# SyncE's loads of the differential heads in written order, with their tiles laid out anew and the clearing moved to VectorE

## The chip, the cores and the metric

The kernel runs on one core of one Trainium2 chip. A core has TensorE (PE, with PEld for the loading of the stationary operand), VectorE (DVE), ScalarE (ACT), GpSimd (POOL) and SyncE (SP, which only issues transfers here). The metric is the device time of one execution in microseconds (us); lower is better. Before the change the median of 3 runs is 2444.63 us (2444.59 to 2448.08).

## The reference, cut to what matters

One layer of a diffusion transformer over 512 latent tokens and 256 context tokens, model width 2048, all in float32. Eight differential attention heads and eight latent-attention heads run on one modulated RMS norm; their outputs go through one projection, and a gated MLP with a short convolution follows. The change lies in the differential heads:

```python
def _diff_attend(q, k, v, lam):
    q1, q2 = jnp.split(q, 2, axis=-1)
    k1, k2 = jnp.split(k, 2, axis=-1)
    s1 = jnp.einsum('bhqd,bhkd->bhqk', q1, k1).astype(jnp.float32) * DA_SCALE
    s2 = jnp.einsum('bhqd,bhkd->bhqk', q2, k2).astype(jnp.float32) * DA_SCALE
    w = jax.nn.softmax(s1, axis=-1) - lam * jax.nn.softmax(s2, axis=-1)
    return jnp.einsum('bhqk,bhkd->bhqd', w.astype(v.dtype), v)
```

Queries are the 512 latent tokens, keys and values all 768 tokens; a head is 128 wide, and q1, q2 and k1, k2 are its halves. Queries and keys carry a rotary embedding.

## The kernel before

**Precision.** A float32 operand is used as two parts, high and low (`split`, lines 75 to 84: a cast on ACT at L80, a subtraction on DVE at L81), and a product as three matmuls (`mm3`, L104 to L106).

**Stages.** Modulation and norms; projections of keys, latent inputs and values, which go to DRAM (`k_d`, `v_d`, `q0_d`; keys by L389, values by L470, the second half of the values through POOL's queue); the differential heads, which are the stage of the change; the latent-attention heads; output projection; MLP. The projection of the values for the second half of the heads is the last work before the differential heads, and the tiles of that time (pools `kv` and `kvs`) are given back when they begin. The pool `da` of the differential heads takes over their memory: `cb1` (8 KB a partition, read by the products with the modulation weights until shortly before), `lt`, `rt`, `qs` and `nq` and others of the latent norms and of the first queries, then the two buffers of the modulation weights, then `kh` and `kl`, through which the values are evacuated. `reuse_waits="tile"` makes a new tile wait only for the old tiles that lie under it.

**One differential head** (`da_head`). Its keys' high parts (`ks`, two buffers), low parts (`klz`, two tiles, used in turn) and values (`v`, two buffers) are loaded. `klz` holds each half's low part in its own 64 partitions and zeros in the other 64; the zeros are written once, by four instructions on POOL (L506). For each of four tiles of 128 queries and each of the two maps, four matmuls make the scores in PSUM (L482, two buffers), DVE takes the maximum (L484), ACT the exponential (L486); then DVE, POOL and DVE normalise and combine the two maps (L538, L539, L540). After the four tiles, for each of six blocks of 128 keys, PE transposes the weights (L494, one PSUM buffer), ACT and DVE split them, and three matmuls add their product with the values (`po`, L104 to L106). ACT copies the sum to `o` (L497), and SP stores it to `o_d` (L544).

**The queries of a head** (`da_queries`). Those of head 0 were made earlier and are loaded from `q0_d` (L515). For the others `feature` multiplies two blocks of query weights (512 KB each) with the 16 tiles of the normed input, 48 matmuls into the PSUM tile `f`; DVE applies the rotary embedding (L149 to L152), and ACT and DVE scale and split (L395, L396). A block is loaded by SP and split by `wblock` (L90). The helper `ahead` runs two blocks ahead in the written program: at the end of `feature` of one head it writes down the loads for the next head. The raw blocks have three buffers (`wr`), the split ones three each (`wh`, `wl`).

**What sets the order.** The program is written head by head,

```python
    for h in range(NH):
        da_head(h, da_queries(h))
```

but a planner decides the order on each engine: at each moment of its own timeline it takes, of the instructions that are ready, the first in written order. On the chip each engine then runs its instructions in that fixed order and waits at each for its semaphores. So a load that is written late can be issued early, if its buffer is free, and PE's instructions of several heads are mixed. Inside a `tc.manual_schedule(engines={...})` block the named engines keep the written order; the last stages of the kernel before use it for PE, ACT, DVE and SP.

Of the kernel before, what the change touches and what calls it, by code (L numbers as in the profile page):

```python
# [9 lines left out]
F32 = mybir.dt.float32  # L10
F32R = mybir.dt.float32r
# [6 lines left out]
P = 128  # L18
D = 2048
KT = D // P  # L20
T = 512
C = 256
TT = T + C
GRID_W = 64
NH = 8
# [7 lines left out]
NKEY = TT // P  # L33
# [19 lines left out]
def layer_kernel(ctx: ExitStack, tc: tile.TileContext, small, rope, c_row, cc_row, x_t, ctx_t, ada, ada_k,  # L53
                 w_g0, w_f, w_v, w_uqn, w_uqr, w_ukv, w_o, w_up0, w_up, w_dn, out_t):
    nc = tc.nc
    pe, ve, sc, gp = nc.tensor, nc.vector, nc.scalar, nc.gpsimd
# [8 lines left out]
    def nm(s):  # L65
        n[0] += 1
        return f"{s}{n[0]}"
# [6 lines left out]
    def b_tile(tag="b", bufs=None):  # L74
        return ps_b.tile([P, 512], F32, tag=tag, name=nm(tag), bufs=bufs or nb[0])
# [62 lines left out]
    q0_d = dram.tile([2, P, T], F32, name="q0_d")  # L138
# [5 lines left out]
    k_d = [dram.tile([2, P, TT], F32, name=f"k_d{h}") for h in range(NH)]  # L144
    v_d = [dram.tile([4, P, 2, NKEY, P], F32, name=f"v_d{i}") for i in range(2)]

    def apply_rope(out, ps, tmp):
        t2 = tmp()
        ve.tensor_tensor(out, ps, ropet[:, 0, :], op=ALU.mult)  # L149
        ve.stream_shuffle(t2, ps, mask=[i ^ 16 for i in range(32)])  # L150
        ve.tensor_tensor(t2, t2, ropet[:, 1, :], op=ALU.mult)
        ve.tensor_tensor(out, out, t2, op=ALU.add)  # L152
# [41 lines left out]
    for row, wide in ((c_row, cb), (cc_row, ccb)):  # L194
        nc.sync.dma_start(wide[0:1], row)
        sc.activation(wide[0:1], wide[0:1], AF.Silu)
        for j in range(0, D, 512):
            t = b_tile()
# [104 lines left out]
    for i in range(2):  # L303
        o = OFF["lam"] + 128 * i
# [11 lines left out]
    for kt in range(KT):  # L316
# [5 lines left out]
        o = (kt % 2) * C  # L322
        hx.append((a2k(F32R), a2k(F32R)))
        hc.append((chh[:, o:o + C], chl[:, o:o + C]))
        with tc.high_priority():
            h = st.tile([P, TT], F32, tag="h", name=nm("h"), bufs=3)
            for i, (x, c, m, (hh, hl)) in enumerate(((xs[kt], slice(0, T), modx, hx[kt]),
                                                     (ct, slice(T, TT), modc, hc[kt]))):
                b, t, r = m[:, kt:kt + 1], h[:, c], rinv[:, c]
# [61 lines left out]
    def stacked_queries(pool, q, scale, bufs=2):  # L391

        qs = [pool.tile([P, T], F32R, tag=f"qs{i}", name=nm("qs"), bufs=bufs) for i in range(2)]
        for i, (r, o) in enumerate(((lo, hi), (hi, lo))):
            sc.mul(qs[i][r], q[r], scale)  # L395
            ve.scalar_tensor_tensor(out=qs[i][o], in0=q[r], scalar=scale, in1=qs[i][r].bitcast(F32),  # L396
                                    op0=ALU.mult, op1=ALU.subtract)
        return qs
# [19 lines left out]
    for i in range(2):  # L418
        t = kv.tile([P, TT], F32, tag="lt", name=nm("ckv"), bufs=3)
# [9 lines left out]
    def feature(lat, ctxo):  # L429
        for hf in range(2):  # L430
            wh, wl = next_block()
            for j in range(8):
                kt = hf * 8 + j
                w = (wh[:, j * P:(j + 1) * P], wl[:, j * P:(j + 1) * P])
                mm3(lat, w, hx[kt], kt == 0, kt == KT - 1)
                if ctxo is not None:
                    mm3(ctxo, w, hc[kt], kt == 0, kt == KT - 1)
        ahead(2)
# [8 lines left out]
    for i in range(3):  # L447
        lat = b_tile()
        feature(lat, None)
        t = kv.tile([P, TT], F32, tag="lt", name=nm("cq"), bufs=3)[:, :T]  # L450
# [4 lines left out]
    for half in range(2):  # L455
        s0, s1, b0, b1_ = s_tile(), s_tile(), b_tile(), b_tile()
        vo = [s0[:, :512], s0[:, 512:], s1[:, :512], s1[:, 512:], b0, b1_]
        for kb in range(8):
            wh, wl = next_block()
            for j in range(2):  # L460
                kt = kb * 2 + j
                w = (wh[:, j * 512:(j + 1) * 512], wl[:, j * 512:(j + 1) * 512])
                for t in range(NKEY):
                    src, o = (hx[kt], t * P) if t < 4 else (hc[kt], (t - 4) * P)
# [13 lines left out]
    def scores_softmax(mms, pool, tag, bufs, l):  # L478
        s = s_tile()
        for c0, c1 in ((0, T), (T, TT)):  # L480
            for i, (a, b) in enumerate(mms):
                pe.matmul(s[:, c0:c1], a, b[:, c0:c1], start=i == 0, stop=i == len(mms) - 1)  # L482
        m = sm.tile([P, 1], F32, tag="m", name=nm("m"), bufs=4)
        ve.tensor_reduce(out=m, in_=s[:, :TT], axis=AX.X, op=ALU.max, negate=True)  # L484
        p = pool.tile([P, TT], F32, tag=tag, name=nm(tag), bufs=bufs)
        sc.activation(p, s[:, :TT], AF.Exp, bias=m, accum_out=l)  # L486
        return p

    def weighted_values(pool, ws, v, dst, last=False):
        po = b_tile("po", 1)  # L490
        for kt in range(NKEY):
            pt = b_tile("f", 2) if last and kt % 3 else b_tile("pt", 1)
            for qt in range(NQT):
                pe.transpose(pt[:, qt * P:(qt + 1) * P], ws[qt][:, kt * P:(kt + 1) * P], ident)  # L494
            wth, wtl = split_tiles(pool, ("wth", "wtl"), [P, T], 2, pt)
            mm3(po, v(kt), (wth, wtl), kt == 0, kt == NKEY - 1)
        sc.copy(dst, po)  # L497


    da = tc.alloc_tile_pool(name="da", bufs=1, reuse_waits="tile")  # L500


    klz = [da.tile([P, 2, TT], F32R, name=nm("klz")) for _ in range(2)]
    for t in klz:
        for i, r in enumerate((hi, lo)):
            gp.memset(t[r, i].bitcast(F32), 0.0)  # L506

    def da_rtmp():
        return da.tile([P, T], F32, tag="rt", name=nm("rt"), bufs=2)

    def da_queries(h):
        if h == 0:
            qs = [da.tile([P, T], F32R, tag=f"qs{i}", name=nm("qs"), bufs=2) for i in range(2)]
            for i in range(2):
                nc.sync.dma_start(qs[i].bitcast(F32), q0_d[i])  # L515
            return qs
        lat = b_tile("f", 2)
        feature(lat, None)
        q = da_rtmp()
        apply_rope(q, lat, da_rtmp)  # L520
        return stacked_queries(da, q, DA_SCALE)

    def da_head(h, qs):
        ks = da.tile([P, 2, TT], F32R, tag="ks", name=nm("ks"), bufs=2)
        kl = klz[h % 2]
        for i, r in enumerate((lo, hi)):
            nc.sync.dma_start(ks[r].bitcast(F32), k_d[h][0].rearrange("(i p) n -> p i n", i=2))
            nc.sync.dma_start(kl[r, i].bitcast(F32), k_d[h][1][r])
        v = da.tile([P, 2, NKEY, P], F32R, tag="v", name=nm("v"), bufs=2)
        nc.sync.dma_start(v.bitcast(F32), v_d[h // 4][h % 4])  # L530
        ws = []
        for qt in range(NQT):
            c = slice(qt * P, (qt + 1) * P)
            l = sm.tile([P, 2], F32, tag="l", name=nm("l"), bufs=4)
            ps = [scores_softmax([(qs[i][:, c], ks[:, i]), (qs[i][:, c], kl[:, i])], da, f"p{i}", (8, 3)[i],
                                 l[:, i:i + 1]) for i in range(2)]
            rl = sm.tile([P, 2], F32, tag="rl", name=nm("rl"), bufs=4)
            ve.reciprocal(rl, l)  # L538
            gp.tensor_scalar(out=ps[1], in0=ps[1], scalar1=rl[:, 1:2], scalar2=neglam, op0=ALU.mult, op1=ALU.mult)  # L539
            ve.scalar_tensor_tensor(out=ps[0], in0=ps[0], scalar=rl[:, 0:1], in1=ps[1], op0=ALU.mult, op1=ALU.add)  # L540
            ws.append(ps[0])
        o = da.tile([P, T], F32, tag="o", name=nm("o"), bufs=2)
        weighted_values(da, ws, lambda kt: (v[:, 0, kt], v[:, 1, kt]), o)
        nc.sync.dma_start(o_d[h], o)  # L544

    for h in range(NH):
        da_head(h, da_queries(h))
    ap_.release()


# [78 lines left out]
    for h in range(NH):  # L629
        i = h % 2  # L630
        if i == 0:
            qs, qn, kn, vs = nxt
# [753 lines left out]
```

## Time and profile before

| what | value |
|---|---|
| median of 3 runs | 2444.63 us |
| the profiled execution | 2446.12 us |
| its span, first to last instruction | 2444.3 us |
| mean granted TensorE clock | 0.99 |
| PE, DVE, ACT, POOL busy | 97%, 71%, 46%, 9% |
| from the end of the value projection to the end of the differential heads | about 478 to 704 us |
| stores of the eight heads' results begin | 538.4 to 701.3 us |

The span is cut into windows, and a view of windows gives for each engine the busy time and, in brackets, the number of instructions. PE's matmuls are pipelined, so that a full row for PE is not yet PE at its peak. In a view of waits each line says which engine's instruction waited for which, for how long in total, how often, and the longest. A row in order of time gives start and duration; "x6" means that rows next to each other were merged, and a duration with the waits inside it is then the whole stretch. "SPq" is SyncE's queue: its rows are the issues of transfers, not the transfers. In groups by line, the two numbers after the bar are the busy time in us and the mean of one instruction in ns.

### The profile page before, as it was taken

The numbers are of one execution on the slowest core, as the hardware profiler recorded it, in microseconds if no ns is written. First come the engines' busy times: TensorE is split into PE (matmuls) and PEld (weight loads), VectorE is DVE, ScalarE is ACT, GpSimd is POOL, SyncE is SP. The second block draws the span as 40 slices with busy tenths as digits, with TensorE's granted clock in tenths as the row PEclk, the third lists the DMA queues.
The fourth block names the chain that finished last, engine by engine and source line by source line (L and its number), as shares of the span: only waits on it lengthen the run. The fifth ranks groups of instructions, "written<-read, shape, count | busy, mean of one in ns | idle before, by whom it ended". The sixth has DMA issues, their size and how long they took to land.

```text
span 2444.3 us, 32956 instructions
## 1 busy us (share of the span) xinstructions
PE 2374.6 (97%) x12790; PEld 1987.4 (81%) x12790; DVE 1730.4 (71%) x2304; ACT 1116.3 (46%) x1700; POOL 221.0 (9%) x244
## 2 busy tenths in 40 slices
PE   7999999999999999999999999999999999999998
PEld 3778887877777778889888888888888888888887
DVE  4668786388868877369766666666666666666667
ACT  4342121155545542245545454545454545454545
POOL 0000000121100002100111111111111111111110
PEclk9999999999999999999999999999999999999999
DMA  7867899555411139523555555565556555555573
GB/s 276 275 238 293 308 339 325 178 179 138 140 59 44 44 147 332 176 87 113 137 140 135 141 135 142 134 143 133 143 132 143 133 141 134 140 135 141 133 191 106
DMA packets 130708, 403.33 MB, mean 165 GB/s; under 512 B 14323, under 2 KB 25075, under 8 KB 122099
## 3 DMA queue, kind: packets, MB, share of 16 engines
q1 hardware_dynamic: 104118, 350.87, 43.8%
q0 software_dynamic: 25280, 49.30, 11.6%
q8 instruction: 100, 1.64, 0.3%
q10 hardware_dynamic: 1152, 1.05, 0.1%
q14 instruction: 58, 0.48, 0.1%
HBM read 331.68 MB, written 69.48 MB: 164 GB/s over the span
## 4 chain that ended last, share of the span: by engine, by line
PE 83%; DVE 8%; ACT 3%; DMA 3%; issue 2%; POOL 1%; SPq 0%; DVEq 0%; ACTq 0%; POOLq 0%
PE y L1105 12%; PE b L104 10%; PE b L105 10%; PE b L106 10%; PE z L1105 6%; PE y L1107 6%; PE z L1107 3%; PE s L104 3%; PE s L105 3%; PE s L106 3%; PE s L482 3%; PE x L1105 2%; DMA ada<-in_ada 1%; PE x L1107 1%; PE f L104 1%
## 5 line engine op out<-in xcount | busy, mean ns | idle before, releaser
L961 DVE TENSOR_TENSOR wl<-wr,wh 128x1024 fp32r<-128x1024 f32 x144 | 176.4, 1225 | 157.1 <-ACT wh L953 156.5
L953 ACT CAST wh<-wr 128x1024 fp32r<-128x1024 f32 x144 | 151.0, 1049 | 233.3 <-PE b L105 119.5
L104 PE MATMUL b<-ah,wh 128*128 128x512 f32 (+1 forms) x664 | 256.8, 387 | 0.0
L105 PE MATMUL b<-al,wh 128*128 128x512 f32 (+1 forms) x664 | 256.7, 387 | 0.0
L106 PE MATMUL b<-ah,wl 128*128 128x512 f32 (+1 forms) x664 | 255.8, 385 | 0.0
L1126 POOL DMA_DIRECT2D x_d<-xs x160 | 139.7, 1003 | 1161.1 <-ACT xs L1125 1158.7
L961 DVE TENSOR_TENSOR wl<-rb,wh 128x1024 fp32r<-128x1024 f32 x123 | 150.1, 1220 | 126.8 <-ACT wh L953 126.8
L953 ACT CAST wh<-rb 128x1024 fp32r<-128x1024 f32 x123 | 129.3, 1051 | 188.3 <-PE b L105 116.1
L961 DVE TENSOR_TENSOR wl<-ws,wh 128x1024 fp32r<-128x1024 f32 x123 | 150.2, 1221 | 89.7 <-ACT wh L953 89.7
L80 ACT CAST wh<-wr 128x1024 fp32r<-128x1024 f32 (+3 forms) x102 | 99.1, 972 | 219.1 <-PE b L106 61.7
L171 DVE CUSTOM_DVE_ANT_0 ada<-ada,cb,smt 128x2048 f32<-128x2048 f32 x64 | 153.4, 2397 | 59.3 <-DMA ada<-in_ada 59.0
L953 ACT CAST wh<-ws 128x1024 fp32r<-128x1024 f32 x123 | 128.2, 1042 | 129.7 <-DVE ws L915 48.6
L1105 PE MATMUL y<-a2k,wh 128*128 128x512 f32 x656 | 164.0, 392 | 0.0
L81 DVE TENSOR_TENSOR wl<-wr,wh 128x1024 fp32r<-128x1024 f32 (+3 forms) x102 | 118.0, 1157 | 53.4 <-ACT wh L80 53.1
L104 PE MATMUL b<-a2k,wh 128*128 128x512 f32 (+1 forms) x376 | 141.7, 377 | 5.9 <-ACT a2k L810 4.3
L106 PEld LDWEIGHTS b<-ah,wl 128*128 128x128 f32 x664 | 124.8, 188 | 25.7
L104 PEld LDWEIGHTS b<-ah,wh 128*128 128x128 f32 x664 | 125.1, 188 | 22.9
L105 PEld LDWEIGHTS b<-al,wh 128*128 128x128 f32 x664 | 125.1, 188 | 22.0
L105 PE MATMUL b<-a2k,wh 128*128 128x512 f32 (+1 forms) x376 | 140.5, 374 | 0.0
L106 PE MATMUL b<-a2k,wl 128*128 128x512 f32 (+1 forms) x376 | 139.3, 371 | 0.0
L1105 PEld LDWEIGHTS y<-a2k,wh 128*128 128x128 f32 x656 | 118.6, 189 | 21.6
L1105 PE MATMUL y<-b2k,wh 128*128 128x512 f32 x410 | 107.8, 393 | 0.0
(449 smaller groups left out, 5770.7 us busy)
## 6 DMA issues: line engine op xcount, KB each, us to landing
ada<-in_ada SPq DMA_DIRECT2D x64, 1024.0 KB, 6.7
rb<-in_w_up SPq DMA_DIRECT2D x123, 512.0 KB, 4.5
wr<-in_w_dn SPq DMA_DIRECT2D x88, 512.0 KB, 4.2
x_d<-xs POOLq DMA_DIRECT2D x160, 256.0 KB, 5.9
wr<-in_w_up SPq DMA_DIRECT2D x53, 512.0 KB, 4.2
wr<-in_w_f SPq DMA_DIRECT2D x34, 512.0 KB, 6.4
adak<-in_ada_k SPq DMA_DIRECT2D x32, 512.0 KB, 6.0
ada<-in_ada SPq DMA_DIRECT2D x32, 512.0 KB, 6.4
```

The source lines that it names most:

```text
L80: sc.copy(dst_h, src)
L81: ve.tensor_tensor(dst_l, src, dst_h.bitcast(F32), op=ALU.subtract)
L104: pe.matmul(out, st[0], mv[0], start=start, stop=False, **kw)
L105: pe.matmul(out, st[0], mv[1], start=False, stop=False, **kw)
L106: pe.matmul(out, st[1], mv[0], start=False, stop=stop, **kw)
L171: ve.tensor_tensor_reduce(out=junk, in0=w, in1=vec, op0=ALU.mult, op1=ALU.add, scale=1.0, scalar=col("b_ada", j), accum_out=dst[:, j:j + 1])
L482: pe.matmul(s[:, c0:c1], a, b[:, c0:c1], start=i == 0, stop=i == len(mms) - 1)
L953: sc.copy(t, raw[:, k * n_:k * n_ + n_])
L961: ve.tensor_tensor(t, raw[:, k * n_:k * n_ + n_], hi[k].bitcast(F32), op=ALU.subtract)
L1105: pe.matmul(o, w[j][0], hs[j], start=start and j == 0, stop=False, skip_group_check=True)
L1107: pe.matmul(o[:, h0], w[j][1], hs[j][:, h0], start=False, stop=j == 7, skip_group_check=True)
L1126: gp.dma_start(x1_d[dt], x, accum_op=ALU.add)
```

## The change

Three edits, all in the stage of the differential heads.

1. The tiles of the pool `da` are asked for in another order. First come the tags `o` and `rt` (2 buffers of 2 KB each, 8 KB together, as much as `cb1`), then `qs0` and `qs1`, then `ks`, and then `klz`; before, `klz` came first, then `qs0`, `qs1`, `ks`. By the sizes in the code, keys and queries of head 0 now lie over `lt`, `rt`, `qs` and `nq`, the tiles `klz` over `nr`, `n1` and the first buffer of the modulation weights, and the values of head 1 end over a buffer of `kh`.
2. The four instructions that clear parts of `klz` run on DVE and not on POOL.
3. Loads get a function of their own (`da_loads`), which is called one head ahead, and SP keeps the written order through the loop: queries of head 0, loads of head 0; then for each head h up to 6 the loads of head h+1, head h with its store, and the queries of head h+1, in which the weight blocks for the queries of head h+2 are loaded. Head 7 itself is written after the block, so that its store is free to be placed.

```diff
     da = tc.alloc_tile_pool(name="da", bufs=1, reuse_waits="tile")
 
+    for tag in ("o", "rt"):
+        da.tile([P, T], F32, tag=tag, name=nm(tag), bufs=2)
+    keys_, vals = {}, {}
+
+    def da_keys(h):
+        keys_[h] = da.tile([P, 2, TT], F32R, tag="ks", name=nm("ks"), bufs=2)
+        return keys_[h]
+
+    qs0 = [da.tile([P, T], F32R, tag=f"qs{i}", name=nm("qs"), bufs=2) for i in range(2)]
+    da_keys(0)
+
     klz = [da.tile([P, 2, TT], F32R, name=nm("klz")) for _ in range(2)]
     for t in klz:
         for i, r in enumerate((hi, lo)):
-            gp.memset(t[r, i].bitcast(F32), 0.0)
+            ve.memset(t[r, i].bitcast(F32), 0.0)
...
     def da_queries(h):
         if h == 0:
-            qs = [da.tile([P, T], F32R, tag=f"qs{i}", name=nm("qs"), bufs=2) for i in range(2)]
             for i in range(2):
-                nc.sync.dma_start(qs[i].bitcast(F32), q0_d[i])
-            return qs
+                nc.sync.dma_start(qs0[i].bitcast(F32), q0_d[i])
+            return qs0
         lat = b_tile("f", 2)
         feature(lat, None)
...
-    def da_head(h, qs):
-        ks = da.tile([P, 2, TT], F32R, tag="ks", name=nm("ks"), bufs=2)
-        kl = klz[h % 2]
+    def da_loads(h):
+        ks = keys_.get(h) or da_keys(h)
         for i, r in enumerate((lo, hi)):
             nc.sync.dma_start(ks[r].bitcast(F32), k_d[h][0].rearrange("(i p) n -> p i n", i=2))
-            nc.sync.dma_start(kl[r, i].bitcast(F32), k_d[h][1][r])
-        v = da.tile([P, 2, NKEY, P], F32R, tag="v", name=nm("v"), bufs=2)
-        nc.sync.dma_start(v.bitcast(F32), v_d[h // 4][h % 4])
+            nc.sync.dma_start(klz[h % 2][r, i].bitcast(F32), k_d[h][1][r])
+        vals[h] = da.tile([P, 2, NKEY, P], F32R, tag="v", name=nm("v"), bufs=2)
+        nc.sync.dma_start(vals[h].bitcast(F32), v_d[h // 4][h % 4])
+
+    def da_head(h, qs):
+        ks, kl, v = keys_[h], klz[h % 2], vals[h]
         ws = []
...
-    for h in range(NH):
-        da_head(h, da_queries(h))
+
+    with tc.manual_schedule(engines={mybir.EngineType.SP}):
+        qs = da_queries(0)
+        da_loads(0)
+        for h in range(NH - 1):
+            da_loads(h + 1)
+            da_head(h, qs)
+            qs = da_queries(h + 1)
+    da_head(NH - 1, qs)
     ap_.release()
```

## The prediction

> **What bounds the kernel now.** I read the page, then the windows and the waits from the end of the value projection (478 us) to the end of the differential heads (704 us), because the diff edits only that stretch.
>
> ```profile
> span 2444.3 us, 32956 instructions
> PE 83%; DVE 8%; ACT 3%; DMA 3%; issue 2%; POOL 1%; SPq 0%; DVEq 0%; ACTq 0%; POOLq 0%
> ```
>
> TensorE sets the end: 83% of the chain is its work, so an idle microsecond of PE there is a lost one. Now the stage: busy time of each engine, granted clock, DMA share.
>
> ```profile
> core 0: us, PE busy (x) PEld busy (x) DVE busy (x) ACT busy (x) POOL busy (x), PEclk, DMA share, GB/s
> 440.00:478.00 38.00, 38.00 (x169) 31.49 (x168) 10.40 (x10) 5.39 (x6) 1.36 (x2) 1.00 0.29 95
> 478.00:493.00 15.00, 10.62 (x47) 8.45 (x45) 5.10 (x7) 4.24 (x6) 7.62 (x11) 0.93 0.92 319
> 546.00:572.00 26.00, 25.86 (x133) 20.03 (x132) 22.33 (x33) 14.94 (x30) 3.85 (x3) 1.00 0.47 135
> 493.00:704.00 211.00, 201.04 (x981) 156.48 (x982) 176.59 (x260) 120.64 (x228) 42.22 (x39) 0.96 0.45 130
> ```
>
> There is one hole (4.4 of the 15 us after 478), where DMA is 0.92 full; then PE is busy 201 of 211 us, with DVE close behind. The waits of PE and of its weight loads name the hole:
>
> ```profile
> PE s L482 <- DMA ks<-k_d: 4.6, 1, 4.6
> ...
> PEld s L482 <- POOL klz L506: 0.6, 1, 0.6
> ```
>
> So head 0's keys come 4.6 us late and the memset of the low parts 0.6 us. That is all the change can win from the waits it names. What keeps PE full afterwards stands in the chain, a stretch in order of time:
>
> ```profile
> 552.08 0.44 PE pt L494 x4
> 552.51 0.23 PE f L106
> 552.98 0.24 PE f L105
> ```
>
> Between the transposes (pt) and products (po) of one head run the matmuls (f) that project a later head's queries, 48 per head at 0.23 us, 11.0 us. They fill every wait for DVE. They can do so only because their weights are there long before; SyncE's queue in order of time shows that:
>
> ```profile
> 440.00 41.17 SPq L90 DMA_DIRECT2D wr<-in_w_f  x6
> 481.22 0.93 SPq L515 DMA_DIRECT2D qs<-q_d  x2
> 493.35 0.34 SPq L90 DMA_DIRECT2D wr<-in_w_f  x1
> 512.51 5.71 SPq L90 DMA_DIRECT2D wr<-in_w_f  x2
> 536.16 0.33 SPq L90 DMA_DIRECT2D wr<-in_w_f  x1
> 538.36 0.33 SPq L544 DMA_DIRECT2D o_d<-o  x1
> 701.31 0.38 SPq L544 DMA_DIRECT2D o_d<-o  x1
> ```
>
> Ten query blocks (two a head, so heads 1 to 5) have been issued before the first head's result is stored at 538.36. From there to the last store the pace is (701.31 - 538.36) / 7 = 23.3 us a head.
>
> **The change, part by part.** *Order of SP.* The block that fixes SP's order issues: queries and loads of head 0, loads of head 1, store of head 0, the two weight blocks for head 2 (written at the end of the query projection of head 1), loads of head 2, store of head 1, blocks for head 3, and so on. Blocks 3 to 10 of those above, and the four that follow them, so all of heads 2 to 7, now stand behind a store. And the store holds the queue; the waits of SP:
>
> ```profile
> SPq L544 <- ACT o L497: 29.2, 7, 24.1
> ```
>
> Seven stores held SP for 29.2 us, one for 24.1, with nothing urgent behind. Now the wait carries a load: the blocks for head h+2 start only when head h is finished. That closes a loop over two heads, priced from these rows:
>
> ```profile
> L484 DVE TENSOR_REDUCE m<-s 128x1 f32<-128x768 f32 x64 | 60.3, 951 | 9.2 <-PE s L482 9.0
> L486 ACT ACTIVATE p<-s,m 128x768 f32<-128x768 f32 x64 | 57.9, 905 | 45.2 <-DVE m L484 41.8 <-issue 1.7 <-ACT p L486 0.9
> L539 POOL TENSOR_SCALAR p<-p,rl,neglam 128x768 f32<-128x768 f32 x32 | 37.6, 1174 | 147.2 <-DVE rl L538 142.1 <-ACT p L486 5.1
> L81 DVE TENSOR_TENSOR wtl<-pt,wth 128x512 fp32r<-128x512 f32 x48 | 33.0, 688 | 10.4 <-ACT wth L80 10.0
> L540 DVE SCALAR_TENSOR_TENSOR p<-p,rl,p 128x768 f32<-128x768 f32 x32 | 32.5, 1016 | 9.5 <-POOL p L539 9.1
> L80 ACT CAST wth<-pt 128x512 fp32r<-128x512 f32 x48 | 27.9, 582 | 18.2 <-PE pt L494 18.0
> L81 DVE TENSOR_TENSOR wl<-wr,wh 128x1024 fp32r<-128x1024 f32 (+2 forms) x17 | 18.8, 1106 | 0.9 <-ACT wh L80 0.8
> L80 ACT CAST wh<-wr 128x1024 fp32r<-128x1024 f32 (+2 forms) x16 | 15.3, 956 | 10.3 <-PE f L105 10.1
> L396 DVE SCALAR_TENSOR_TENSOR qs<-rt,qs 64x512 fp32r<-64x512 f32 x14 | 10.3, 735 | 1.1 <-ACT qs L395 0.7
> L395 ACT ACTIVATE qs<-rt 64x512 fp32r<-64x512 f32 x14 | 8.8, 628 | 3.5 <-DVE rt L152 3.3
> L152 DVE TENSOR_TENSOR rt<-rt,rt 128x512 f32<-128x512 f32 x7 | 5.7, 818 | 0.1
> L497 ACT COPY o<-po 128x512 f32<-128x512 f32 x8 | 4.7, 587 | 9.0 <-PE po L106 9.0
> ...
> wr<-in_w_f SPq DMA_DIRECT2D x9, 512.0 KB, 5.9
> ```
>
> Store and two issues 3 x 0.33 = 1.0; landing 5.9; first cast 1.0; projection 11.0; rotation, four DVE instructions of 0.7 to 0.8, 2.9, then the scaled halves 0.63 + 2 x 0.735 = 2.1; softmax 0.7 for the first scores, DVE 8 x 0.951 + 4 x 1.016 + 4 x 0.16 = 12.3, and the last tile's exponential (0.9 + 0.2) and POOL step 1.2, together 15.3; weighted values, through one PSUM buffer, 6 x (0.44 + 0.58 + 0.69) = 10.3, then the last products 0.7 and the copy 0.6, 11.6. Sum 50.8 us if the other head never stands in the way. It does: its transposes and products come first on PE, 6 x (0.44 + 3 x 0.23) = 6.8, and its DVE work of 6 x 0.69 (low parts) + 2 x 1.1 (weights) + 4.4 (rotation and queries) = 10.7 falls partly into this head's softmax. That part is between 0 and 10.7; DVE is busy 22 of 26 us today, so I take 10. Loop: 50.8 + 6.8 + 10 = 67.6 us for two heads, against 46.6 today. From store 0 to store 6 there are three loops, then a last step of today's 23.3 (head 7's store is outside the fixed order and nothing waits behind it): 226.1 against 163.0, **+63.1 us**.
>
> *Start.* SP reaches head 0's loads right after head 1's two blocks, not after six, and the new layout puts keys and queries over tiles that the latent norms and old queries leave; so they land before 478, in a stretch where DMA is 0.29 busy. Gone: 5.2 us of waits. Next late is the evacuation of the values into the buffers that the scores need. The projection of heads 2 and 3, mixed into head 0 today, is missing too, so store 0 comes sooner. The last projection before the hole, in order of time on PE, is
>
> ```profile
> 488.23 0.39 PE L106 MATMUL f<-a2k,wl 128*128 128x512 f32 x1
> ```
>
> so the earliest is 488.6 + 15.3 + 11.6 = 515.5, which is 22.9 before 538.4; at the least 5.2 sooner. I take **-13**, near the middle, because scores of head 1 share DVE.
>
> *Memsets.* Four of 0.73 us move from POOL to DVE. Before 478 DVE is busy 10.4 of 38 us, which hides them; placed behind the last value evacuation they cost up to the nearest DVE row of that width, 2 x 0.951 = 1.9, ahead of the first maximum. Taken as 0. On POOL they stood behind the value stores; nothing else there moves.
>
> *Layout and loads a head ahead.* Head 1's values lie over buffers that the value stores drain until about 493; the wait blocks SP, but behind it stands store 0, which waits longer. Probabilities lie over such buffers too: 0 to 2 us, taken as 0. Keys and values of head h+1 no longer come late, and of those waits the trace shows only head 0's: 0 more.
>
> *Clock.* PE keeps its 201 us of work in a longer stage, so it idles each head. What idling costs is seen twice in short windows:
>
> ```profile
> 490.00:492.00 2.00, 0.00 (x0) 0.00 (x0) 0.50 (x1) 1.53 (x2) 0.99 (x2) 0.71 1.06 380
> 494.00:496.00 2.00, 1.94 (x6) 1.65 (x7) 0.67 (x1) 0.00 (x0) 1.84 (x4) 0.50 1.00 396
> 680.00:682.00 2.00, 1.12 (x6) 0.69 (x5) 1.94 (x4) 0.52 (x1) 0.98 (x1) 1.00 0.00 0
> 686.00:688.00 2.00, 2.00 (x9) 1.71 (x8) 0.42 (x1) 0.45 (x2) 0.00 (x0) 0.50 0.35 98
> ```
>
> After the 4.6 us hole, and after a merely thin stretch near 680, the clock is 0.50 for some 6 us, 3 us of PE time lost. Some 12 such places (two a head, heads 2 to 7) make 0 to 36 us; PE stands on the loop for less than a third of it (17.8 of 67.6), so I take **+10**. [...]
>
> **Sum.** -13 + 63.1 + 10 = +60.1 on the profiled execution's 2446.1 (span 2444.3 and 1.8 around it; median 2444.6): **2506 us**.
>
> **Rivals.** *The written order hides the loads.* One mechanism: the loop is shorter than two heads' present pace, 46.6 us; then nothing waits and only the start counts, -5.2 and the 3 us of half clock after the hole: 2438 us. For it: landings can be quicker than 5.9, and keys have two buffers. Against it: 50.8 without any sharing, since a free weight buffer is filled only once the store has let go. [...]
>
> *Two heads out of step.* The loop runs at its floor, one head's softmax under the other's projection: 3 x 50.8 + 23.3 = 175.7, +12.7, less 13: 2446 us, no change. Against it: PE and DVE take work in program order, so the earlier head goes first.
>
> *The start is not gained.* The planner may release the new memory only after the value evacuations, as SP's order today suggests (four blocks for heads 2 and 3 were issued ahead of queries that wait for nothing); then the hole and its half clock stay, and 8 of the 13 us are lost: 2514 us. A part that doesn't do what it says.
>
> **How the numbers follow.** Forecast 0.75, hidden loads 0.10, out of step 0.08, start not gained 0.07. The forecast's own range is 2475 to 2540: loop sharing 6.8 to 17.5, clock 0 to 36, start -5 to -23. The range 2455 to 2542 leaves out the two light cases and the worst clock. A measurement here can tell 0.2% (4.9 us) from no change. Faster 0.12, same 0.05, slower 0.83.
>
> **What would show it.** Right: SP's wait of the store for the copy of o several times 29.2 us; casts of the query weights, or PE's projections, waiting for the DMA of wr; PE holes of some us per head between 510 and 740 and clock rows of 0.5; stores in pairs with long steps between; no wait of the first scores for ks. Wrong: the stores keep 23 us a head, or the weight blocks for head 2 are issued ahead of store 0.

## The result, and the profile after

The changed kernel takes 2506.24 us (median of 5 runs, 2503.89 to 2514.52) against 2444.63 (5 runs, 2442.74 to 2448.08): a ratio of 1.0264, with a 95% interval of 1.0251 to 1.0278. The forecast was 2506.0. The profiled execution took 2506.1 us, its span and the chain's shares by engine are

```profile
span 2504.1 us, 32919 instructions
...
PE 85%; DVE 6%; ACT 4%; DMA 3%; issue 2%; POOL 0%; SPq 0%; DVEq 0%; ACTq 0%; POOLq 0%
```

TensorE still sets the end. SyncE's queue in order of time (start, length, line) shows the written order at work: the queries of head 0 leave at 447.76, where they left at 481.22 before, and every pair of weight blocks stands right behind a store.

```profile
438.40 9.31 SPq L90 DMA_DIRECT2D wr<-in_w_f  x2
447.76 0.90 SPq L527 DMA_DIRECT2D qs<-q_d  x2
...
523.62 0.33 SPq L558 DMA_DIRECT2D o_d<-o  x1
523.99 0.93 SPq L90 DMA_DIRECT2D wr<-in_w_f  x2
...
541.45 0.33 SPq L558 DMA_DIRECT2D o_d<-o  x1
...
594.75 0.33 SPq L558 DMA_DIRECT2D o_d<-o  x1
...
664.34 0.33 SPq L558 DMA_DIRECT2D o_d<-o  x1
...
736.06 0.32 SPq L558 DMA_DIRECT2D o_d<-o  x1
759.70 0.33 SPq L558 DMA_DIRECT2D o_d<-o  x1
```

Store 0 is 14.7 us earlier than before (523.62 against 538.36). Then the even stores, heads 0, 2, 4 and 6, are 71.1, 69.6 and 71.7 us apart, and the last step is 23.6. From the first store to the last it is 236.1 us, where it was 163.0: 73.1 more. (A second trace of the changed kernel, from a later run, has store 0 at 526.17 and 232.5 us from there to the last store.) Less the 14.7 of the start, the last store is 58.4 us late; the two spans differ by 59.8. So the whole loss lies in this stage. The waits (engine, line and tile, what it waited for: us, times, longest), SyncE's from 470 to 780 us and the others' from 478 to 780:

```profile
SPq L558 <- ACT o L497: 200.6, 8, 48.7
```

```profile
ACT wh L80 <- DMA wr<-in_w_f: 24.8, 11, 5.1
PE pt L494 <- DVE p L554: 21.2, 16, 2.9
PE f L104 <- ACT wh L80: 7.7, 5, 3.9
```

The stores now hold SyncE for 200.6 us instead of 29.2, and what stands behind them is late: the casts of the query weights wait for their loads (24.8 us), and TensorE's projections for the casts. The wait of the first scores for the keys is no longer in the list. The windows of the same stage:

```profile
478.00:493.00 15.00, 11.92 (x55) 9.40 (x54) 10.25 (x17) 4.62 (x9) 6.62 (x9) 1.00 0.58 212
493.00:520.00 27.00, 19.60 (x86) 13.94 (x87) 23.55 (x35) 16.61 (x33) 6.74 (x6) 0.94 0.00 0
520.00:546.00 26.00, 23.91 (x95) 16.97 (x94) 8.29 (x12) 7.26 (x11) 0.98 (x1) 0.80 0.60 172
572.00:598.00 26.00, 18.61 (x76) 13.12 (x76) 17.92 (x26) 13.43 (x26) 4.54 (x5) 0.83 0.09 27
478.00:760.00 282.00, 230.60 (x1020) 170.45 (x1019) 185.53 (x270) 126.92 (x233) 40.06 (x42) 0.92 0.35 104
```

and the whole stage in the kernel before:

```profile
478.00:704.00 226.00, 211.66 (x1028) 164.92 (x1027) 181.70 (x266) 124.88 (x234) 49.84 (x49) 0.96 0.48 143
```

With nearly as many matmuls, TensorE is busy 230.6 of 282 us instead of 211.7 of 226. So 51.4 us are idle instead of 14.3, and it is busy 18.9 us longer, at a granted clock of 0.92 instead of 0.96. The start of the stage is not tighter either: from 478 to 520 us TensorE is idle for 10.5 us (3.1 and 7.4 in the first two rows), where it was 5.2 before.

One turn of the loop can be followed in the chain (start, length, what), from the store of head 2 to that of head 4:

```profile
594.75 0.33 SPq L558
595.18 4.57 DMA wr<-in_w_f
599.77 1.05 ACT wh L80
600.86 0.80 PE f L104
...
614.92 0.33 SPq L558
...
615.85 6.32 DMA wr<-in_w_f
622.19 1.06 ACT wh L80
623.27 1.23 DVE wl L81
624.50 0.61 DVE rt L152
...
626.53 0.98 PE s L482 x4
...
645.24 0.49 PE pt L494
...
664.34 0.33 SPq L558
```

and the projection of head 4 ends on TensorE with

```profile
618.23 0.39 PE L106 MATMUL f<-a2k,wl 128*128 128x512 f32 x1
```

The store lets the blocks of head 4 go; the first of them has landed at 599.75; the projection runs from 600.86 to 618.6; the first scores come at 626.53, the first transpose that has all its probabilities at 645.24, the store at 664.34. The lines at 614.92 to 624.50 show a side way that the prediction did not have: head 4's rotation (rt) stands behind a low part (wl) on VectorE, which is of head 5's blocks, and those have just come from behind the store of head 3.

### The profile page after: what moved, and what is told of

It reads as the page before. It is cut to its first block, busy times and chain, and to the rows that moved or that the text cites. A ratio compares the mean times of both kernels' runs of the same rounds, so it can differ in the third digit from the quotient of the medians.

```text
span 2504.1 us, 32919 instructions
## 1 busy us (share of the span) xinstructions
PE 2395.1 (96%) x12790; PEld 1996.1 (80%) x12790; DVE 1731.4 (69%) x2308; ACT 1118.5 (45%) x1700; POOL 213.4 (9%) x240
## 4 chain that ended last, share of the span: by engine, by line
PE 85%; DVE 6%; ACT 4%; DMA 3%; issue 2%; POOL 0%; SPq 0%; DVEq 0%; ACTq 0%; POOLq 0%
PE y L1126 12%; PE b L105 10%; PE b L104 10%; PE b L106 10%; PE z L1126 6%; PE y L1128 6%; PE s L105 3%; PE s L104 3%; PE s L106 3%; PE z L1128 3%; PE s L482 3%; PE x L1126 2%; PE pt L494 1%; PE f L104 1%; PE x L1128 1%
```

## The experiments

Each time stands beside runs of the kernel before on the same chip. The medians of before were 2442.8 (store on GpSimd, store one place later, order alone, blocks loaded twice), 2443.0 (places and memsets alone, memsets alone, order for the start), 2443.1 (values behind the blocks, blocks of head 2 first, order for the start again) and 2444.5 (changed kernel and order alone, side by side).

**The store on another queue.**

```diff
-        nc.sync.dma_start(o_d[h], o)
+        gp.dma_start(o_d[h], o)
```

> The changed kernel, but the store of each head's result is issued by GpSimd instead of SyncE; SyncE's order is else the same. Theory (the store at the head of SyncE's queue keeps the weight blocks back and closes a loop over two heads, 67.6 us predicted, 71 us between every other store in the changed kernel's trace): the blocks of head h+2 now stand behind the values of head h+1 only, which wait for the end of head h-1, so the loop takes three heads, some 71 us for three, about TensorE's own 23.3 a head. Time 2433 to 2446 us, stores evenly 23 to 24 us apart. Rival 1 (not the store, but the loads a head ahead, the moved memory or the memsets cost the time): 2500 us or more, stores in pairs. Rival 2 (the values' wait simply takes over the store's part): 2470 to 2506 us, SyncE waits for the values' buffer about as long as it waited for the stores, 200 us.

2461.96 us, ratio 1.0084 (1.0068 to 1.0100). Two thirds of the loss are gone by moving one instruction to another queue, which speaks against rival 1. But 19 us stay, so the theory's time is missed. Rival 2 names rightly what takes over the store's part, the values' wait, but it is 113.1 us and not 200, and the time lies below its 2470. The place where SyncE waits, and the copies of the results on ScalarE, one a head (heads 0 to 5):

```profile
SPq L541 <- PE po L106: 113.1, 6, 25.0
```

```profile
523.51 0.59 ACT L497 COPY o<-po 128x512 f32<-128x512 f32 x1 [0.55 <-PE po L106]
542.74 0.59 ACT L497 COPY o<-po 128x512 f32<-128x512 f32 x1 [0.73 <-PE po L106]
574.44 0.59 ACT L497 COPY o<-po 128x512 f32<-128x512 f32 x1 [0.71 <-PE po L106]
605.67 0.59 ACT L497 COPY o<-po 128x512 f32<-128x512 f32 x1 [0.55 <-PE po L106]
631.41 0.59 ACT L497 COPY o<-po 128x512 f32<-128x512 f32 x1 [0.73 <-PE po L106]
659.73 0.59 ACT L497 COPY o<-po 128x512 f32<-128x512 f32 x1 [1.92 <-PE po L106]
```

Now the load of the values (L541) holds the queue until the head before last has been read. A block of head h+3 follows the end of head h: a loop over three heads, as expected. Three heads take 82.2, 88.7 and 85.3 us, though, not 71. The expectation had carried the sharing with one other head over from the loop of two; in a loop of three there are two others. With 16.8 us for each, 50.8 + 2 x 16.8 = 84.4.

**The store one place later on SyncE.**

```diff
-        nc.sync.dma_start(o_d[h], o)
+        return o
...
-            da_head(h, qs)
+            o = da_head(h, qs)
             qs = da_queries(h + 1)
+            nc.sync.dma_start(o_d[h], o)
```

> The changed kernel, with one line moved: the store of head h is written after the queries of head h+1, so behind the weight blocks of head h+2 and not ahead of them; it stays on SyncE. Theory: only the place in the queue counts, so the time is that with the store on GpSimd within 5 us, 2433 to 2446 us. Rival 1 (a store on SyncE costs wherever it stands, for its wait blocks the queue): about 2470 to 2506 us, because the loads of head h+2 still stand behind it. Rival 2 (the store has nothing to do with it): 2506 us.

2466.28 us, ratio 1.0094 (1.0079 to 1.0109): 4.3 us above the store on GpSimd, so within the 5 us named, and again some 20 us above the range, for the same reason. That is also 4 us below the range of rival 1. The store still waits on SyncE (149.4 us in seven waits from 430 to 720), with the loads of head h+2 and the blocks of head h+3 behind it, but no longer the blocks of head h+2. So a blocked queue was cheap or dear here by what stands behind the blocking instruction.

**The values behind the blocks.** With the store on GpSimd, and the values' load moved behind the blocks, the loop spans four heads.

```diff
...
             qs = da_queries(h + 1)
+            da_values(h + 1)
...
```

(da_values holds the two lines of da_loads that allocate and load the values.)

> The kernel with the stores on GpSimd, and besides the load of the values of head h+1 written behind the weight blocks of head h+2 instead of ahead of them. The blocks of head h+2 then stand behind the values of head h only, which wait for the end of head h-2: a loop over four heads. Theory (a head costs 50.8 us alone, and each other head inside its loop adds its share of TensorE and VectorE, 6.8 + 10 = 16.8 us): two heads 67.6, three 84.4 (28.1 a head; the runs with three showed 82 to 89 us, 27.2 a head), four 101.2, so 25.3 a head against 23.3 before, 12 us more from the first store to the last, less 8 at the start: 2445 to 2451 us. Rival 1 (from four heads on nothing waits any more): 2433 to 2441 us. Rival 2 (what costs the time in the runs with three heads is not the loop but the lowered clock and sharing, which stay): 2458 to 2466 us.

2447.09 us, ratio 1.0012 (1.0003 to 1.0021), inside the range of the theory. The copies of heads 0, 1, 4 and 5:

```profile
523.77 0.59 ACT L497 COPY o<-po 128x512 f32<-128x512 f32 x1 [0.65 <-PE po L106]
547.50 0.59 ACT L497 COPY o<-po 128x512 f32<-128x512 f32 x1 [1.30 <-PE po L106]
...
624.57 0.59 ACT L497 COPY o<-po 128x512 f32<-128x512 f32 x1 [3.03 <-PE po L106]
654.37 0.59 ACT L497 COPY o<-po 128x512 f32<-128x512 f32 x1 [1.82 <-PE po L106]
```

Four heads take 100.8 and 106.9 us (101.2 expected). The last copy starts at 698.4, 174.6 after the first: 11.6 more than before between stores, 12 expected. A part of the time is not the stage's: by the traces it ends about 2 us earlier than before, and the span is still 1 us longer (2445.3 against 2444.3; the medians are 4 apart). From 704 to 730 TensorE is busy 22.4 us here and 24.5 before, with a wait of 2.8 us for the next stage's keys. So the pace of the loop agrees with the theory, while the total agrees partly by what came behind.

**The blocks loaded twice.**

```diff
-        nc.sync.dma_start(raw[:, :cols], src)
+        for _ in range(2 if twice else 1):
+            nc.sync.dma_start(raw[:, :cols], src)
...
```

> The changed kernel, but each of the twelve weight blocks of heads 2 to 7 is loaded twice into the same tile, the second load behind the first, so that the blocks land about 5 and 10 us later and everything else stays. Theory (the landing of the blocks is a link of a loop that is walked three times): 5 to 9 us more each time, 2521 to 2533 us, stores two apart 76 to 80 us instead of 71. Rival (TensorE's work and its lowered clock set the pace, the loads are hidden behind it): 2506 to 2511 us.

2511.71 us, ratio 1.0276 (1.0259 to 1.0294), about 5.5 above the changed kernel's 2506.24, so just above the rival's range and far from the theory's. Even the 5.5 are not a clear difference. The two did not run side by side, and their ratios to before agree within their intervals; beside this run the order alone (below), which has the same loop, took 2511.21, and on another chip 2503.72. SyncE's and TensorE's rows of the same turn (heads 2 to 4):

```profile
596.16 0.33 SPq L561 DMA_DIRECT2D o_d<-o  x1
596.53 9.13 SPq L91 DMA_DIRECT2D wr<-in_w_f  x4
```

```profile
606.73 0.77 PE L105 MATMUL f<-a2k,wh 128*128 128x512 f32 x1
...
624.63 0.39 PE L107 MATMUL f<-a2k,wl 128*128 128x512 f32 x1
629.28 0.50 PE L485 MATMUL s<-ks,qs 128*128 128x512 f32 x1 [4.26 <-DVE qs L399]
```

From store to first product it is 10.6 us instead of 6.1, so the delay did get into the loop, 4.5 us in this turn. But from the end of the projection to the first scores it is 4.3 us instead of 7.9: head 5's blocks are late as well, so their low part no longer stands ahead of head 4's rotation on VectorE (it runs at 630.37, behind the queries). 3.6 of the 4.5 us were given back within the turn, which is 72.4 us long instead of 69.6. The rival's mechanism, loads that lie beside other work, is not what this turn shows; the theory's size was wrong here because the two heads' chains cross on VectorE. (That four issues hold SyncE for 9.13 us, where two took 0.93, is the second load's wait for the first, which writes the same tile: the view of SyncE's waits has 43.3 us for loads of such blocks from 430 to 720 us, in twelve waits, the longest 4.3.) In sum the three turns are 3.8 us longer than the changed kernel's (216.2 against 212.4); the four traces of this loop without second loads, two of the changed kernel and two of the order alone, range from 206.0 to 212.4. The other two turns were not taken apart link by link, so what a later landing costs in the whole loop stays open.

**The order alone.** The written order and the loads a head ahead, with the old places and the memsets on GpSimd; against the changed kernel:

```diff
-    for tag in ("o", "rt"):
-        da.tile([P, T], F32, tag=tag, name=nm(tag), bufs=2)
...
-    qs0 = [da.tile([P, T], F32R, tag=f"qs{i}", name=nm("qs"), bufs=2) for i in range(2)]
-    da_keys(0)
...
-            ve.memset(t[r, i].bitcast(F32), 0.0)
+            gp.memset(t[r, i].bitcast(F32), 0.0)
```

The tiles are allocated where they are first used, as before.

> The kernel before with the written order of SyncE and the loads a head ahead, but with the old places in memory and the memsets on GpSimd. Theory: the order alone makes the loop, so from the first store to the last it takes 236 us as in the changed kernel; the earlier start needs the memory too, so the hole in TensorE's work of 4 to 5 us stays ahead of the first scores, and the time is 2511 to 2519 us. Rival 1 (the order alone brings the earlier start, the new places bring nothing): 2503 to 2509 us, no hole. Rival 2 (the new places or the memsets on VectorE make a part of the loss): under 2500 us.

2511.21 us, ratio 1.0280 (1.0265 to 1.0295), just inside the theory's range. From the first store to the last it takes 234.7 us, as the theory said. But the start is the rival's:

```profile
478.00:493.00 15.00, 14.33 (x65) 11.40 (x63) 6.31 (x10) 4.56 (x9) 11.47 (x16) 1.00 0.53 212
```

No hole: TensorE is busy 14.3 of the 15 us with the old places. To settle which holds, this kernel and the changed one stood side by side on one chip:

> The changed kernel once more, beside the written order with the old places and GpSimd's memsets, on the same chip: 2504 to 2508 us. If the new places and the memsets bring a part of the early start (theory), it is 3 to 8 us faster than the other; if the order alone does (rival), the two are within 2 us.

> The written order with the old places and GpSimd's memsets once more, beside the changed kernel on the same chip. Theory (places and memsets bring a part of the early start): 2509 to 2514 us. Rival (the order alone brings it, and the 5 us between the first two runs were two chips): within 2 us of the changed kernel, 2504 to 2508 us.

2505.54 us (ratio 1.0248, 1.0224 to 1.0272) for the changed kernel, 2503.72 (1.0240, 1.0220 to 1.0260) for the order alone. Within 2 us: the rival. From the first store to the last the traces of this pair have 232.5 and 229.6 us. The order makes both the early start and the loss; the new places and VectorE's memsets bring nothing that can be measured.

**The places and memsets alone, and the memsets alone.** The first takes the written order out of the changed kernel, and SyncE's instructions stand as in the kernel before; the second makes one change to the kernel before.

```diff
-    with tc.manual_schedule(engines={mybir.EngineType.SP}):
...
+    for h in range(NH):
+        qs = da_queries(h)
+        da_loads(h)
+        da_head(h, qs)
```

```diff
-            gp.memset(t[r, i].bitcast(F32), 0.0)
+            ve.memset(t[r, i].bitcast(F32), 0.0)
```

> The kernel before with the new places in memory for keys and queries and with VectorE's memsets, but without a written order: SyncE's instructions stand as in the kernel before, four weight blocks of heads 2 and 3 ahead of the first queries. Theory (the first keys are late because they stand behind those blocks in the queue, not because of their memory): the hole of about 4.6 us before the first scores stays; 2442 to 2447 us, no change. Rival (the memory alone lets them in): hole gone, 5 to 8 us less, 2436 to 2440 us.

> The kernel before with one change: the four memsets of the low parts on VectorE instead of GpSimd. Theory: VectorE has room for them ahead of the first scores and GpSimd's were covered but for 0.6 us of TensorE's weight loads: 2443 to 2446 us, no change. Rival 1 (they stand ahead of the evacuation of the values and the first maximum): 1 to 3 us more. Rival 2 (GpSimd's place behind the value stores held the low keys' loads back): 2 to 5 us less.

2446.46 us (ratio 1.0011, 1.0002 to 1.0020) and 2443.64 (1.0002, 0.9993 to 1.0011): both within the 0.2%, the first by 3.5 us slower than before. With the new places the hole before the first scores stays (5.1 us), so the memory alone does not let the keys in. With the memsets alone on VectorE, TensorE's wait from 470 to 500 us reads

```profile
PE s L482 <- DVE klz L506: 4.7, 1, 4.7
```

The hole is still there and only its name is another. The first memset ends at 491.00 and comes last, but by the trace the second part of head 0's keys has landed only at 490.86: the keys were late all the same. It was the queue, with four weight blocks ahead of head 0's loads: in the kernels with the written order the wait is gone, with the old places and with the new.

**The order for the start alone.** The written order ends after the blocks of head 3; later loads and all stores are left to the planner.

```diff
     with tc.manual_schedule(engines={mybir.EngineType.SP}):
-        qs = da_queries(0)
+        qs = [da_queries(0)]
         da_loads(0)
-        for h in range(NH - 1):
-            da_loads(h + 1)
-            da_head(h, qs)
-            qs = da_queries(h + 1)
+        o = da_head(0, qs[0])
+        qs.append(da_queries(1))
+        da_loads(1)
+        qs.append(da_queries(2))
...
```

> The changed kernel's memory and memsets, with SyncE's order written for the start alone: queries and loads of head 0, blocks of head 2, loads of head 1, blocks of head 3; all later loads and all stores are left to the planner. Theory: the start's gain of the changed kernel (hole of 4.6 us, 0.6 us of weight loads, some 3 us of half clock) comes without the loop: 2433 to 2441 us, stores from the first to the last 163 us apart or a little more. Rival 1 (the first store was early in the changed kernel only because the projections of heads 2 and 3 were missing ahead of it, and the rest comes back later): 2442 to 2446 us. Rival 2 (an order written for a part pushes the blocks of later heads behind a wait again): over 2450 us.

> The kernel with the order written for the start alone once more, beside the one with the blocks first, on the same chip: 2436 to 2442 us, faster than before by 1 to 8 us as at first (2439.9 against 2443.0); a time equal to before within 1 us would say that the first difference was chance.

2439.94 us (ratio 0.9990, 0.9980 to 0.9999) and 2440.34 (0.9988, 0.9979 to 0.9997): faster than before by some 3 us, twice, the only version that beats both kernels, and by less than the 0.2% that one measurement was said to tell. It is in the theory's range of 2433 to 2441 at its upper end. In the two traces store 0 is 10.7 and 7.9 us earlier than before (527.68 and 530.48), the last store 8.1 and 4.7 (693.23 and 696.57). So about 3 us of the early first store come back on the way, as they would if a part of the projections of heads 2 and 3, which the kernel before runs inside head 0, is put off and not saved. (The trace of before is of an execution of 2446.12 us, 3 above the medians of before beside these two, so these differences are on the high side.) And a new wait stands at the start; the rows are from the second of the two traces, TensorE's longest wait and then the windows:

```profile
491.03 0.50 PE L482 MATMUL s<-ks,qs 128*128 128x512 f32 x1 [1.67 <-ACT p L486]
```

```profile
488.00:490.00 2.00, 1.35 (x7) 0.80 (x5) 1.80 (x4) 0.02 (x1) 0.00 (x0) 1.00 0.97 324
490.00:492.00 2.00, 0.97 (x5) 0.76 (x5) 2.00 (x5) 2.00 (x5) 0.00 (x0) 1.00 0.87 342
492.00:494.00 2.00, 1.20 (x4) 0.76 (x4) 1.80 (x4) 1.77 (x4) 0.98 (x1) 0.59 0.01 4
494.00:496.00 2.00, 1.74 (x5) 1.45 (x6) 2.00 (x3) 1.84 (x4) 0.00 (x0) 0.50 0.00 0
496.00:498.00 2.00, 2.00 (x8) 1.61 (x7) 1.30 (x4) 0.20 (x3) 0.00 (x0) 0.50 0.39 129
```

The first softmax is late next, nothing is there to fill it, and the clock falls from 1.00 to 0.50, as it did after the old hole (0.50 from 492 to 496 us in the kernel before).

**The blocks of head 2 ahead of head 0's values.**

```diff
         qs = [da_queries(0)]
         da_loads(0)
         qs.append(da_queries(1))
+        da_values(0)
         o = da_head(0, qs[0])
...
```

> The kernel with the order written for the start alone, with one change: the two blocks of head 2 stand ahead of the values of head 0 in SyncE's queue, not behind them. The trace without it shows a wait of 1.7 us of TensorE at 488 us for the exponential of the first scores, with no projection at hand to fill it, and the clock at 0.50 from 490 to 496. Theory: with the blocks issued before the values are free (482.7 us) the projection of head 2 fills that wait, the clock stays at 1.00, and 3 to 5 us go: 2433 to 2438 us. Rival 1 (a block needs a weight buffer that is free only later anyway): no difference to the run without it, 2438 to 2442 us. Rival 2 (projections ahead of the first scores only delay head 0): 2 to 5 us more than without it.

2449.56 us, ratio 1.0023 (1.0013 to 1.0033): 9 us more than the same order with the values first, on the same chip. Rival 2, and worse. TensorE's wait:

```profile
484.62 0.79 PE L104 MATMUL f<-a2k,wh 128*128 128x512 f32 x1 [6.35 <-DVE kl L81]
```

The first matmul of a projection stands in TensorE's order where it has to wait 6.35 us for the last but one of VectorE's evacuations of the values, and the matmuls behind it wait too; the clock is 0.50 from 484 to 488. The filler became the hole.

## Why the prediction was right, and where it was not

*The loop over two heads* is what the change costs, and it is settled: the changed order alone has it, a store that is moved takes 40 to 44 us of it away, and with one head more in the loop each time the pace goes from 35.4 us a head (212.4 / 6) to 28.5 (mean of three) to 26.0 (mean of two), toward the 23.3 of the kernel before. The sum was +63.1 and +10 for the clock, 73.1; the trace has 73.1. That the two agree to the tenth is luck: the second trace has 69.5. So is the total of 2506, for the 60.1 was added to the profiled execution's 2446.1 and not to the median of 2444.63. The links of the turn shown compare like this:

| link | predicted | heads 2 to 4 |
|---|---|---|
| store, issues, landing | 6.9 | 5.0 |
| first cast | 1.0 | 1.1 |
| projection, with the other head's transposes and products | 11.0 + 6.8 | 17.8 |
| rotation, queries | 5.0 | 7.9 |
| softmax | 15.3 | 18.7 |
| weighted values, copy | 11.6 | 19.1 |
| VectorE shared, clock | 10 + 3.3 | in the three rows above: 13.8 |
| sum | 70.9 | 69.6 |

So the mechanism and the sum hold, but two terms are only confirmed together: of the 13.8 us, the traces don't part what VectorE's other work and what the halved clock cost. Over the stage TensorE is busy 18.9 us longer, and an estimate puts about 11 of these down to the clock: by windows of 2 us it works for 35.6 us at a clock of 0.50, 13.7 before, and half of the difference is lost, for there a projection's matmul takes 0.43 us (at 601.66 in the chain) instead of 0.23. How much of the 11 lay on the path was not measured, and the predicted 10 stays unproved. The count under it was too high: between 510 and 740 us there are six stretches at 0.50, not 12 places. And the sharing is not where it was put: the largest piece is not in the softmax but in the weighted values (7.5 us), which run beside the next head's scores; a further 2.9 us is the rotation behind the next head's low parts.

*Start*, -13 predicted, -14.7 at store 0, -12.2 in the second trace. The size holds, the reason only by half. The wait for the keys went because the queue was reordered. That "the new layout puts keys and queries over tiles that the latent norms and old queries leave" had no part in it: the order alone does as well with the old places. And TensorE idles more ahead of store 0, not less (10.5 us from 478 to 520 instead of 5.2), because the waits of the first softmax have no projection to fill them. What makes store 0 early is the other half of the reason, the projections of heads 2 and 3 that are missing: from 478 us to store 0 TensorE has 38 matmuls of projections instead of 133, and 95 x 0.23 is 21.9 us. That is work put off, which the loop, counted from store 0, then had to carry. A gain that lasts is some 3 us, by the medians of the order for the start alone.

*Memsets*, 0 predicted; alone they change nothing (ratio 1.0002). *Layout and loads a head ahead*, 0 predicted; the changed kernel and the order alone are within 2 us.

*The rivals.* Hidden loads: in the changed kernel the casts wait 24.8 us for the loads. Two heads out of step: the turn holds the other head's products in full. Start not gained: no wait of the first scores for the keys. All three fell, and the signs named came as named: SyncE's wait for the copies 6.9 times 29.2 us, stores in pairs, clock rows of 0.50 (from 522 to 530 us, for one). The forecast's own range doesn't follow from its terms, whose ends give 2456 to 2542 us and not 2475 to 2540; and 2542, the upper end of the wider range, holds the worst clock that it was said to leave out. Neither matters at 2506.

*Double buffers.* Each tile that is loaded has its second or third buffer here, in all the kernels above. The buffers alone did not decide whether a load is there in time. From 470 to 720 us the kernel before shows no wait of a cast for the load of query weights; the changed kernel, up to 780 us, shows 24.8 us of them. What decided was whether the queue lets a load go: with unchanged buffers the time lies anywhere between 2440 and 2511 us by the place of stores and loads in the queues.

## What to carry to other kernels

When an order of loads is written out, look at each instruction that waits for a result and ask what stands behind it in the queue: here a store at the head of a queue turned "one head ahead" into a loop over two heads, of 69.6 to 71.7 us, against 46.6 for two heads before; such a loop's length, with every other head's share of the engines in it, has to be shorter than the work of as many heads. A first result that comes earlier is no gain by itself (the first store 14.7 us earlier, the last 58.4 later); see whether work was put off, and what is late next. Where two waits end almost together (490.86 and 491.00 us with the memsets alone), the profile names only the last, and a wait that gets another name need not have another cause.

## What the runs showed of the hardware

A lower clock came after a matmul stream that was merely thin. In the second trace of the order for the start no wait of TensorE from 486 to 500 us is longer than 1.67 us, and it is busy 2.3 of the 4 us from 488 to 492; the clock falls in the window after that (0.59) and is 0.50 from 494 to 498.
